# Hybrid NSA and gated DeltaNet block on one core: the padding tile in front of the activations grows from 224 to 288 bytes

## The chip, the cores and the metric

The kernel runs on one core of one Trainium2 chip. The metric is the device time in microseconds (us) of one execution. The engines are called by their short names: PE (TensorE, the products), PEld (its loading of weights), DVE (VectorE), ACT (ScalarE), POOL (GpSimd) and SP (SyncE, which issues most transfers).

## The reference

One layer of a decoder block over 256 tokens of 2,048 features, in float32. Cut to what matters here, it is a chain of large products with small mixers between them:

```python
proj = rms_norm(x, norm1_w) @ w_in
o_nsa = nsa_mixer(...)        # attention: compressed, selected and window branch, 8 heads
o_dn = gated_deltanet(...)    # linear attention, 8 heads, chunks of 64
mixed = g_nsa * (o_nsa @ w_up_nsa) + g_dn * (o_dn @ w_up_dn)
x = x + mixed @ w_o
h2 = rms_norm(x, norm2_w)
x = x + (silu(h2 @ w_ffn_gate) * (h2 @ w_ffn_up)) @ w_ffn_down
return rms_norm(x, norm_f_w)
```

All weights come from main memory, mostly 512 KB per transfer, and each is used for all 256 tokens at once. The hidden width of the FFN is 5,632.

## The kernel before

**How a product is made.** Every float32 operand is split into two parts, hi and lo, in the type that PE multiplies in one pass (float32r); a product of two operands is made of hi x hi, hi x lo and lo x hi. Weights arrive in six buffers called raw, ACT writes hi (L171), DVE writes lo = raw - hi (L172). There are three buffers hi of 4,096 bytes per partition and three buffers lo of 4,352. Activations are split once per stage and stay in memory for the whole of it.

**Two kinds of groups.** A product on PE has a stationary operand (128 columns, loaded as weights, PEld) and a moving operand that is streamed past it.
- `group_t` (transposed groups) holds hi or lo of the weights stationary and streams 256 tokens of activations. Its products are L248. Half a chunk is 24 of them: 16 with hi and 8 with lo. It makes most of the input projection (activations `hh`), the two up projections (`odn`, `onsa`) and the FFN's gate and up (`h2`, shown as `h` in the trace).
- Natural groups hold activations stationary and stream 512 columns of hi or lo: `products` (L1307, L1308, L1312) for `w_o` (activations `xa`, `leftw`) and for the FFN's down projection (`fa`, `fx`, `comb`, `leftsy`, `left1`, and the tiles `dd`), and `nat_mm` (L276, L277, L278) for the first groups (`zab`, 354 and 356 columns wide) and for `nsav`, with `hh` stationary. In some units seven products of blocks stand in place of eight; their combined weights are staged through main memory by the generator `staged`, in the tiles `stagew` and `stage`.
- The last products of all (`last_half`, L1663 to L1665) stream 256 columns of a tile `dd` past `fx`.

**The nudge.** After some transposes and other plain products the flag `nudge` is set. The next half chunk of `group_t` then writes its lo 16 elements (64 bytes) further into the buffer (the third argument of `split`, L242); the buffer has the room for it.

**The order of work.** PE's order is the order of the program. Small work (mixers, staging) stands in generators that `pump` advances by one step after each half chunk; `staged` lets six pumps pass between asking for a load and using it.

**Where the tiles lie.** Tiles are placed one behind the other along each partition, pool by pool, in the order of the pools: `wp` (raw, hi, lo), `cp` (constants, then the pad, then two tiles R), `sp` (small values), `hp` (`hh`, later `xa`, later `fa`: one piece of memory), `xy` (four tiles x, y, z, w that change their use), then `arena` (the mixers' memory) and in its place `pb` (`h2`, later `comb`; `dd`; temporaries). The pad is a tile that nothing reads or writes. By the sizes, with the pad at 56 floats, the addresses modulo 256 bytes are:

| behind the pad? | tiles | address modulo 256 |
|---|---|---|
| no | hi, lo | 128 |
| no | lo, nudged | 192 |
| yes | hh, h2, odn, onsa | 0 |
| yes | xa, fa, fx, comb | 64 |
| yes | leftw (two of three), leftsy, left1, dd, stage | 0 |
| yes | arena's main, stagew, x1t | 64 |

`hh` and `fa` share one piece of memory, but `four` starts `hh` at its beginning and `xa` and `fa` 16 elements further; `h2` and `onsa` are moved by 48 elements within their tiles, which start at 64.

Of the kernel before, what the change touches and what calls it, by code (L numbers as in the profile page):

```python
# [7 lines left out]
F32 = mybir.dt.float32  # L8
# [6 lines left out]
P = 128  # L15
# [84 lines left out]
class Kern:  # L100
# [885 lines left out]
    def build(self):  # L986
# [54 lines left out]

        xT = self.ar.alloc([16, 256], "x")
        sq = self.ar.alloc([4, 4, 256], "y")
        self.cp.tile([P, 56], F32, name="pad")
        hh = self.four(self.hp, "a", "hh", 16, 0)

        class First:
# [881 lines left out]
```

## Time and profile before

| what | value |
|---|---|
| median of 3 executions | 1484.56 us (1484.2 to 1484.64) |
| the profiled execution's own time | 1485.05 us |
| its span | 1483.3 us |
| PE busy | 1472.5 us, 99% |
| DVE, ACT, POOL busy | 1076.6, 749.2, 69.5 us |
| moved by DMA | 363.70 MB, 245 GB/s in the mean |

The span goes from the first instruction of the program to the last; the time of an execution has a little around it. Busy times count an engine's instructions where they overlap only once. The chain of work that ended last is followed back from the last instruction, at each step to what released it; its shares say which engine and line set the end. In the groups of instructions the mean length of a product is that of one in a pipeline, from its start to its modelled end; several are under way at a time, so the distance between two starts is shorter. In the list in order of time, each row has the start, the length, and how many instructions in succession were merged.

### The profile page before, as it was taken

The numbers are of one execution on the slowest core, as the hardware profiler recorded it, in microseconds if no ns is written. First come the engines' busy times: TensorE is split into PE (matmuls) and PEld (weight loads), VectorE is DVE, ScalarE is ACT, GpSimd is POOL, SyncE is SP. The second block draws the span as 40 slices with busy tenths as digits, with TensorE's granted clock in tenths as the row PEclk, the third lists the DMA queues.
The fourth block names the chain that finished last, engine by engine and source line by source line (L and its number), as shares of the span: only waits on it lengthen the run. The fifth ranks groups of instructions, "written<-read, shape, count | busy, mean of one in ns | idle before, by whom it ended". The sixth has DMA issues, their size and how long they took to land.

```text
span 1483.3 us, 27316 instructions
## 1 busy us (share of the span) xinstructions
PE 1472.5 (99%) x10937; PEld 1408.1 (95%) x10937; DVE 1076.6 (73%) x1645; ACT 749.2 (51%) x945; POOL 69.5 (5%) x62
## 2 busy tenths in 40 slices
PE   9999999999999999999999999999999999999997
PEld 9999999999999999998899999999999999888886
DVE  7668997767797755677876766666666556968777
ACT  6655444344445445445654444444344445766666
POOL 1000101000000000120000000000000000000000
PEclk9999999999999999999999999999999999999999
DMA  8765556357766457658778888888888655898895
GB/s 292 229 202 172 176 169 199 130 169 238 262 226 213 142 188 251 216 180 274 261 271 297 318 310 306 303 300 313 307 315 304 228 184 184 272 325 279 273 319 207
DMA packets 108462, 363.70 MB, mean 245 GB/s; under 512 B 12192, under 2 KB 12848, under 8 KB 104240
## 3 DMA queue, kind: packets, MB, share of 16 engines
q1 hardware_dynamic: 93264, 293.17, 58.7%
q10 hardware_dynamic: 13968, 66.17, 12.2%
q0 software_dynamic: 1104, 2.64, 0.7%
q8 instruction: 85, 1.39, 0.4%
q14 instruction: 41, 0.34, 0.1%
HBM read 327.57 MB, written 34.35 MB: 244 GB/s over the span
## 4 chain that ended last, share of the span: by engine, by line
PE 99%; DMA 0%; DVE 0%; SPq 0%; ACT 0%; issue 0%; DVEq 0%
PE mm L248 68%; PE mm L1307 6%; PE mm L1308 6%; PE mm L1312 6%; PE mm L277 2%; PE mm L276 2%; PE mm L278 2%; PE oacc L943 1%; PE U L613 1%; PE mmx L1312 1%; PE mmx L1308 1%; PE mmx L1307 1%; DMA raw<-in_zab 0%; PE pt L929 0%; PE hid L796 0%; PE hid L797 0%
## 5 line engine op out<-in xcount | busy, mean ns | idle before, releaser
L171 ACT ACTIVATE hi<-raw 128x1024 fp32r<-128x1024 f32 (+2 forms) x390 | 407.2, 1045 | 520.3 <-PE mm L248 413.5
L172 DVE TENSOR_TENSOR lo<-raw,hi 128x1024 fp32r<-128x1024 f32 (+2 forms) x390 | 469.9, 1205 | 232.8 <-ACT hi L171 231.2
L248 PE MATMUL mm<-h,hi 128*128 128x256 f32 x2816 | 363.4, 281 | 0.0
L248 PEld LDWEIGHTS mm<-h,hi 128*128 128x128 f32 x2816 | 346.6, 188 | 0.1
L248 PE MATMUL mm<-hh,hi 128*128 128x256 f32 x2304 | 300.3, 283 | 0.0
L248 PEld LDWEIGHTS mm<-hh,hi 128*128 128x128 f32 x2304 | 283.7, 188 | 0.6 <-ACT hi L171 0.4
L1288 DVE TENSOR_TENSOR lo<-raw,hi 128x1024 fp32r<-128x1024 f32 (+1 forms) x177 | 196.9, 1131 | 60.8 <-ACT hi L1287 56.5
L1287 ACT ACTIVATE hi<-raw 128x1024 fp32r<-128x1024 f32 (+1 forms) x177 | 173.1, 986 | 99.6 <-PE mm L1308 60.8
L248 PE MATMUL mm<-h,lo 128*128 128x256 f32 x1408 | 195.7, 281 | 0.0
L248 PEld LDWEIGHTS mm<-h,lo 128*128 128x128 f32 x1408 | 179.3, 188 | 0.0
L248 PE MATMUL mm<-hh,lo 128*128 128x256 f32 x1152 | 160.3, 281 | 0.0
L248 PEld LDWEIGHTS mm<-hh,lo 128*128 128x128 f32 x1152 | 146.7, 188 | 0.0
L1550 POOL TENSOR_TENSOR sgt<-sgt,R 128x512 f32<-128x512 f32 x22 | 35.3, 1603 | 546.9 <-ACT sgt L1549 546.9
L276 PE MATMUL mm<-hi,hh 128*128 128x354 f32 (+2 forms) x128 | 44.0, 350 | 1.2 <-ACT hi L158 1.2
L277 PE MATMUL mm<-lo,hh 128*128 128x354 f32 (+2 forms) x128 | 44.4, 347 | 0.0
L278 PE MATMUL mm<-hi,hh 128*128 128x354 f32 (+2 forms) x128 | 44.0, 344 | 0.0
L1307 PE MATMUL mm<-hi,fa 128*128 128x512 f32 x112 | 44.0, 393 | 0.0
L1308 PE MATMUL mm<-hi,fa 128*128 128x512 f32 x112 | 44.0, 392 | 0.0
L1307 PE MATMUL mm<-hi,comb 128*128 128x512 f32 x91 | 35.9, 394 | 0.0
L1308 PE MATMUL mm<-hi,comb 128*128 128x512 f32 x88 | 34.5, 392 | 0.0
L1400 POOL TENSOR_TENSOR main<-main 128x512 f32<-128x512 f32 x7 | 15.1, 2158 | 394.0 <-DVE main L1399 394.0
L248 PE MATMUL mm<-onsa,hi 128*128 128x256 f32 x256 | 33.0, 281 | 0.0
(550 smaller groups left out, 1745.7 us busy)
## 6 DMA issues: line engine op xcount, KB each, us to landing
raw<-in_wfg SPq DMA_DIRECT2D x176, 512.0 KB, 5.3
raw<-in_wmg SPq DMA_DIRECT2D x64, 512.0 KB, 3.7
raw<-in_wd SPq DMA_DIRECT2D x64, 512.0 KB, 5.2
raw<-in_wdn SPq DMA_DIRECT2D x48, 512.0 KB, 4.2
stage<-in_wd ACTq DMA_DIRECT2D x48, 512.0 KB, 6.8
scrD<-stage ACTq DMA_DIRECT2D x24, 1024.0 KB, 6.5
raw<-in_nsa SPq DMA_DIRECT2D x32, 512.0 KB, 3.5
raw<-in_wo SPq DMA_DIRECT2D x26, 512.0 KB, 4.9
```

The lines of the kernel that those rows point to most:

```text
L171: nc.scalar.activation(hv, v, AF.Copy)
L172: nc.vector.tensor_tensor(lv, v, hv.bitcast(F32), op=OP.subtract)
L248: nc.tensor.matmul(ps[:, f], (hv, hv, lv)[p][:, k, f * P:f * P + P], a[:, p % 2, :], start=c + h + p + k == 0, stop=c == n - 1 and h + p + ...
L276: nc.tensor.matmul(o, a[:, 0, sl], hv[:, k, :], start=begin, stop=False)
L277: nc.tensor.matmul(o, a[:, 0, sl], lv[:, k, :], start=False, stop=False)
L278: nc.tensor.matmul(o, a[:, 1, sl], hv[:, k, :], start=False, stop=last)
L1287: keep(nc.scalar.activation(hv, v, AF.Copy))
L1288: keep(V.tensor_tensor(lv, v, hv.bitcast(F32), op=OP.subtract))
L1307: nc.tensor.matmul(bank, ahi, hv[:, k, :], start=id(bank) not in begun, stop=False)
L1308: nc.tensor.matmul(bank, alo, hv[:, k, :], start=False, stop=False)
L1312: nc.tensor.matmul(bank, ahi, lv[:, k, :], start=False, stop=end)
L1550: nc.gpsimd.tensor_tensor(sgt[:], sgt[:], self.R2b, op=OP.mult)
```

## The change

The pad gets 16 floats more, 64 bytes per partition. Everything allocated behind it, that is R, the small values, the activations, the mixers' memory and the tiles that later take its place, moves by 64 bytes. raw, hi and lo and the first constants (`ident`, `n2t`, `ones`, `warm`, `n1t`) stay. `hh`, `h2`, `odn` and `onsa` then lie at 64 modulo 256 and `xa`, `fa`, `fx` and `comb` at 128. No instruction is added or removed.

```diff
         xT = self.ar.alloc([16, 256], "x")
         sq = self.ar.alloc([4, 4, 256], "y")
-        self.cp.tile([P, 56], F32, name="pad")
+        self.cp.tile([P, 72], F32, name="pad")
         hh = self.four(self.hp, "a", "hh", 16, 0)
```

## Prediction

> **What bounds the kernel now.** I read the first part of the page, then the chain of work that ended last, then single products on TensorE.
>
> ```profile
> PE 1472.5 (99%) x10937; PEld 1408.1 (95%) x10937; DVE 1076.6 (73%) x1645; ACT 749.2 (51%) x945; POOL 69.5 (5%) x62
> ...
> PEclk9999999999999999999999999999999999999999
> ...
> PE 99%; DMA 0%; DVE 0%; SPq 0%; ACT 0%; issue 0%; DVEq 0%
> PE mm L248 68%; PE mm L1307 6%; PE mm L1308 6%; PE mm L1312 6%; PE mm L277 2%; PE mm L276 2%; PE mm L278 2%; PE oacc L943 1%; PE U L613 1%; PE mmx L1312 1%; PE mmx L1308 1%; PE mmx L1307 1%; DMA raw<-in_zab 0%; PE pt L929 0%; PE hid L796 0%
> ```
>
> TensorE is never idle and its clock is granted in full. The span is therefore the number of products times the distance between the starts of two of them, which I call the pace. No engine or transfer beside TensorE sets the end, and the change removes no product. It can only change the pace. The time by line says where: L248, the transposed groups, has 68%; lines 1307, 1308 and 1312, the natural groups, some 20%.
>
> The pace of L248 comes from the chain of waits, which gives a long unbroken stretch as one piece, and the number of products from the busy time of that line over the whole span:
>
> ```profile
> 758.07 489.86 PE mm L248 x4128
> ```
> ```profile
> 0.00:1483.30 1483.30, 1014.97 (x8448) 1.00 0.72 245
> ```
>
> 489.86 us over 4,128 products is 118.67 ns each. 256 columns at this pace, and 8,448 such products in all, make 1,002 us. The length that the groups show for one product (281 ns) is a pipelined length and not the pace.
>
> **Which addresses meet.** A product streams its moving operand while the weights (the stationary operand) of the next one are loaded. I write "distance" for the address of the moving operand minus that of the stationary one, modulo 256 bytes. By the sizes of the tiles, laid end to end, hi and lo (all in front of the pad) start at 128; behind the pad hh, h2, odn and onsa start at 0, xa, fa, comb and fx at 64, leftw, leftsy, left1 and the dd tiles at 0. Everything behind the pad moves by 64, hi and lo stay.
>
> - L248 streams activations (0) past hi or lo (128): distance 128, which becomes 192.
> - Lines 1307 to 1312 stream hi or lo (128) past fa, xa, comb or fx (64): 64 becomes 0. Past leftw, leftsy, left1 and dd: 128 becomes 64.
> - A nudged lo starts at 192, so its distance 64 becomes 128.
>
> The trace of before has products at the new distances, since a few pair two tiles behind the pad. They keep their own distance and serve as samples.
>
> **Distance 192 at 256 columns** is what L248 will have. The last twelve products (dd streamed at 0 past fx at 64) run at it. First and last in order of time:
>
> ```profile
> 1473.02 0.28 PE L1663 MATMUL mmx<-dd,fx 128*128 128x256 f32 x1
> ...
> 1474.31 0.28 PE L1665 MATMUL mm<-dd,fx 128*128 128x256 f32 x1
> ```
>
> Eleven steps in 1.29 us are 117.3 ns; two digits behind the point leave 116.4 to 118.2. The nearest other row is a nudged group (distance 64), eight steps from 227.79 to 228.73, 117.5 ns:
>
> ```profile
> 227.79 1.10 PE L248 MATMUL mm<-hh,lo 128*128 128x256 f32 x8
> 228.73 0.52 PE L248 MATMUL mm<-hh,hi 128*128 128x256 f32 x3
> ```
>
> I take 117.7, in the upper half of the rows' interval since twelve products are few. That is 0.97 ns less for each of 8,448: **-8.2 us**. The lower bound is 116.4, or -19.2 us. The upper bound is the slowest pace that 256 columns show anywhere over eight steps or more, here at distance 128:
>
> ```profile
> 540.13 1.12 PE L248 MATMUL mm<-hh,hi 128*128 128x256 f32 x8
> 541.09 1.12 PE L248 MATMUL mm<-hh,lo 128*128 128x256 f32 x8
> 542.05 0.64 PE L248 MATMUL mm<-hh,hi 128*128 128x256 f32 x4
> ```
>
> Twice 0.96 us over eight are 120.0 ns, 1.33 more than now: +11.2 us for all.
>
> **512 columns.** Two stretches of 132 products each, both over comb and fa, so at the same addresses (distance 64); then 27 steps of distance 128, eight of distance 0 (comb streamed at 64 past fx at 64) and six of distance 192:
>
> ```profile
> 1289.24 0.40 PE L1307 MATMUL mm<-hi,comb 128*128 128x512 f32 x1
> ...
> 1320.04 0.39 PE L1307 MATMUL mm<-hi,dd 128*128 128x512 f32 x1
> ...
> 1402.88 0.39 PE L1307 MATMUL mm<-hi,comb 128*128 128x512 f32 x1
> ...
> 1433.10 0.39 PE L1307 MATMUL mm<-hi,dd 128*128 128x512 f32 x1
> ```
> ```profile
> 1272.56 0.39 PE L1307 MATMUL mm<-hi,left 128*128 128x512 f32 x1
> ...
> 1278.86 0.39 PE L1307 MATMUL mm<-hi,fa 128*128 128x512 f32 x1
> ...
> 1464.32 0.62 PE L1312 MATMUL mm<-comb,fx 128*128 128x512 f32 x2
> ...
> 1466.13 0.39 PE L1307 MATMUL mm<-dd,fx 128*128 128x512 f32 x1
> ...
> 1467.53 0.39 PE L1307 MATMUL mmx<-hi,fa 128*128 128x512 f32 x1
> ```
>
> 30.80 us over 132 are 233.3 ns, 30.22 us are 228.9: one distance holds either of two paces for a whole stretch, whichever it fell into. Distance 128: 6.30 us over 27, 233.3. Distance 0: 1.81 us over eight, 226.3 (225.0 to 227.5 by its digits). Distance 192: 1.40 us over six, 233.3. So the distance matters, and 0 has the shortest pace seen. How many of the products these are is read from the groups of L1307, which 1308 and 1312 repeat:
>
> ```profile
> L1307 PE MATMUL mm<-hi,fa 128*128 128x512 f32 x112 | 44.0, 393 | 0.0
> L1307 PE MATMUL mm<-hi,comb 128*128 128x512 f32 x91 | 35.9, 394 | 0.0
> L1307 PE MATMUL mm<-hi,xa 128*128 128x512 f32 x83 | 32.7, 394 | 0.0
> L1307 PE MATMUL mm<-hi,fx 128*128 128x512 f32 x33 | 12.9, 391 | 0.0
> L1307 PE MATMUL mm<-hi,leftsy 128*128 128x512 f32 x26 | 10.2, 394 | 0.0
> L1307 PE MATMUL mm<-hi,leftw 128*128 128x512 f32 x26 | 10.3, 396 | 0.0
> ```
>
> The first four are 319, three lines 957, and some 10% more write the bank that the trace calls mmx: about 1,050 go from 64 to 0. I take 229.6 for now (between 228.9 and 233.3, nearer the first) and 226.9 for then, in the upper half again: -2.7 x 1,050 = **-2.8 us**. If they lock at 233.3 instead: +3.9 us. The others, with left1 and dd about 250, and 96 of nsav, go from 128 to 64: 233.3 to 229.6, **-1.3 us**, with +0 as the bound where they stay at 233.3.
>
> **The rest.** The 288 products of 354 and 356 columns in zab alternate between two distances, 128 and 8 or 16:
>
> ```profile
> 43.04 0.33 PE L276 MATMUL mm<-hi,hh 128*128 128x356 f32 x1
> ...
> 44.02 0.32 PE L276 MATMUL mm<-hi,hh 128*128 128x356 f32 x1
> ...
> 44.98 0.60 PE L1084 MATMUL R<-ident,rstd 128*128 128x128 f32 x4
> ```
>
> Six steps take 0.98 us (163 ns), the next six 0.96 (160). Their new distances are 64 and about 200; I take nothing, with 3 ns either way as bounds, +-0.9 us. Plain fp32 products between two tiles behind the pad keep their distance. ACT and DVE have the same instructions, and TensorE covers them. DMA destinations behind the pad move too: stage from 0 to 64. stagew lies at 64 already:
>
> ```profile
> stage<-in_wd ACTq DMA_DIRECT2D x48, 512.0 KB, 6.8
> stagew<-in_wo ACTq DMA_DIRECT2D x4, 512.0 KB, 7.2
> ```
>
> 0.4 us more for a load is hidden by the six pumps that the generator waits, each 24 products of 118.67 ns, 17 us together. If that cover went, 48 loads would cost 19 us at most. The Trainium skill ("DMA: Bandwidth & Descriptors", section "How a descriptor splits into AXI transactions") says that a descriptor which doesn't start on a 256-byte boundary takes an additional transaction; the 0.4 us agrees in sign, and it leaves the sum as it is.
>
> **The sum.** -8.2 - 2.8 - 1.3 = -12.3 us. The profiled execution took 1485.05 us (span 1483.3 and 1.75 around it), 0.5 above the median of 1484.56. From its time 1472.8, from the median 1472.3. First products after every restart don't hold the pace yet; I write 1473.
>
> **Rivals.**
> *A worse lock (slower).* L248 falls, at a restart after transposes, into the 120.0 pace or its like and stays for the stretch, as the 132 products at 233.3 did. For it: 512 columns at distance 192 show the slowest pace, 233.3; one stretch of L248 has 4,128 products, so one bad start decides half; and the nudge, which ahead of some stretches now changes the distance to 64 for eight products, will change it to 128, where the 120.0 was seen. Against it: at 256 columns of L248's rows only this one stretch of some 20 products is quoted with it, against 4,128 without, and the twelve at distance 192 did not have it. Price: +11.2 - 4.1 = 1491.6 us; with 233.3 in the 512 columns too, 1499.6. It decides once more than 0.6 of L248's products run so (12.3 of 8.2 + 11.2).
>
> *No change.* The paces belong to the stages and their history, not to addresses, or the pad is swallowed by rounding. For it: hh, h2, odn and onsa, four tiles, have one pace, but they also have one address modulo 256. Against it: comb past fx takes 226.3 where dd past fx, the same shapes a moment later, takes 233.3. Rounding can't swallow it, since the tiles behind the pad stand at odd multiples of 64 too. Time: 1484.6. The Trainium skill ("SBUF — State Buffer", section "Who interferes with whom") gives TensorE two independent read ports, one for the moving operand and one for weights, and says it never waits on anyone. By that rule the addresses could not matter and the change would do nothing; the pair of rows just named disagrees.
>
> *Half of it.* L248 gains 8.2, the 512 columns lock at 233.3 (+3.9, +0): 1480.3 us.
>
> **Chances.** Forecast 0.50, half of it 0.10, no change 0.10, worse lock 0.27; 0.03 for a mixture of both signs, a third to each side. A measurement of this kernel tells 0.2% (3 us) from no change. Faster 0.61, same 0.11, slower 0.28. The forecast's own range is 1464 (116.4 for L248 would give 1461.3) to 1478. The range that leaves out no more than 2 in 10 goes up to the worse lock with its price: 1465 to 1493.
>
> **What would show it.** The stretch of L248 that now is x4128 with 489.86 us would be 486 at 117.7 and 495 at 120.0, and unchanged if addresses don't matter. The 132 products over comb and fa would take 29.95 us at 226.9. TensorE would stay at 99% in the chain; a share of DMA there above 0% would say that the faster stream uncovered the loads, and I would be wrong in calling them hidden. The forecast falls if the long stretch is longer than 489.9.

## The result and the profile after

The changed kernel takes 1441.75 us (median of 5 executions, 1441.32 to 1444.0). The kernel before, on the same chip and between them, takes 1484.2 us (1483.82 to 1484.64). The ratio is 0.9717, with a 95% interval of 0.9702 to 0.9731: 42 us or 2.8% faster. The forecast was 1473.0 with a range down to 1465, so the sign is right and the size is not: the gain is more than three times the 12 us that were worked out. The profiled execution took 1441.32 us, with a span of 1439.5.

The page of the changed kernel: busy times, and the chain that ended last by engine and line.

```profile
PE 1428.2 (99%) x10937; PEld 1366.6 (95%) x10937; DVE 1075.0 (75%) x1645; ACT 748.5 (52%) x945; POOL 69.7 (5%) x62
...
PE 97%; DVE 1%; DMA 1%; ACT 0%; issue 0%; SPq 0%; DVEq 0%; ACTq 0%
```

The same products, with TensorE as busy as before: what fell is the pace. The span by three stages (up to the long stretch of L248, that stretch, and the rest), first of the kernel before and then of the changed one. A row has the stretch, its length, then the busy time and number of instructions of PE, PEld, DVE, ACT and POOL, the granted clock, the DMA's share and GB/s:

```profile
0.00:758.07 758.07, 755.94 (x5821) 733.19 (x5822) 577.52 (x1073) 389.46 (x541) 34.23 (x40) 1.00 0.63 210
758.07:1247.93 489.86, 489.86 (x4129) 489.86 (x4129) 315.40 (x347) 206.45 (x214) 35.27 (x22) 1.00 0.82 285
1247.93:1483.30 235.37, 226.66 (x990) 185.10 (x989) 183.69 (x226) 153.27 (x191) 0.00 (x0) 0.99 0.81 276
```
```profile
0.00:739.11 739.11, 736.51 (x5821) 713.86 (x5822) 576.54 (x1073) 388.89 (x541) 34.27 (x40) 1.00 0.64 215
739.11:1207.09 467.98, 467.98 (x4129) 467.98 (x4129) 315.38 (x347) 206.62 (x214) 35.46 (x22) 1.00 0.85 299
1207.09:1439.50 232.41, 223.68 (x990) 184.73 (x989) 183.12 (x226) 153.01 (x191) 0.00 (x0) 0.99 0.83 279
```

The clock is granted in full in both. The saving is 18.96 us before the long stretch, 21.88 in it, and 2.96 in the natural groups behind it, 43.8 together. By line, over the whole span of the changed kernel, L248 (busy time of that line, products, clock, DMA):

```profile
0.00:1439.50 1439.50, 974.05 (x8448) 1.00 0.74 253
```

That is 40.9 us less than the 1014.97 of before. So L248 alone has 93% of the saving of the profiled executions. Its pace is read from the chain, for the kernel before and for the changed one (start, length, number):

```profile
61.40 60.00 PE mm L248 x504
566.86 91.12 PE mm L248 x768
```
```profile
61.07 57.40 PE mm L248 x504
413.82 5.66 PE mm L248 x48
...
425.91 5.46 PE mm L248 x48
...
551.98 87.33 PE mm L248 x768
739.11 467.98 PE mm L248 x4128
```

The long stretch now has 467.98 / 4,128 = 113.37 ns per product, where 117.7 was forecast. The stretches of 48 show two paces side by side: 5.66 / 48 = 117.9 and 5.46 / 48 = 113.8. The forecast's sample, the twelve products dd past fx, still has the slower one in this very execution, first and last in order of time:

```profile
1429.19 0.28 PE L1663 MATMUL mmx<-dd,fx 128*128 128x256 f32 x1
...
1430.49 0.28 PE L1665 MATMUL mm<-dd,fx 128*128 128x256 f32 x1
```

Eleven steps take 1.30 us, 118 ns. Distance 192 thus has at least two paces at 256 columns, and the sample showed the one that most of L248 did not take.

The switch can be seen. Around the start of the long stretch (after), four plain products for R are followed by 16 products with hi, the eight with the nudged lo, and the rest:

```profile
738.86 2.13 PE L248 MATMUL mm<-h,hi 128*128 128x256 f32 x16
740.83 1.11 PE L248 MATMUL mm<-h,lo 128*128 128x256 f32 x8
741.78 1.88 PE L248 MATMUL mm<-h,hi 128*128 128x256 f32 x15
```

Eight nudged products take 0.95 us (118.8 ns). By the starts in the trace, the first step of the stretch takes 200 ns and the next 14, ahead of the nudge, 117.9 each. From the fourth product behind the nudged ones to the end, 4,100 steps, each takes 113.33.

The natural groups went as forecast. The 132 products over comb and fa, first product and the one behind the last:

```profile
1247.88 0.39 PE L1307 MATMUL mm<-hi,comb 128*128 128x512 f32 x1
...
1277.79 0.39 PE L1307 MATMUL mm<-hi,dd 128*128 128x512 f32 x1
```

29.91 us over 132 are 226.6 ns; the forecast had 29.95. In the list of what TensorE waited for, the changed kernel has one row that the kernel before has not (us in total, times, longest):

```profile
...
PE x1T L1435 <- DVE x1t L1427: 0.8, 1, 0.8
```

The transposes of x1T now come 0.8 us before DVE has finished x1t. No wait on a transfer is in the list, though loads land later than before (stage 7.1 us in place of 6.8). The chain passes through one more load, near the end. The row of the issues, and that of the chain:

```profile
stage<-in_wd ACTq DMA_DIRECT2D x48, 512.0 KB, 7.1
```
```profile
1407.25 6.86 DMA raw<-in_wd
```

### The profile page after: what moved, and what is told of

Same layout as the page of the kernel before. It is cut to its first block, busy times and chain, and to the rows that moved or that the text cites. A ratio compares the mean times of both kernels' runs of the same rounds, so it can differ in the third digit from the quotient of the medians.

```text
span 1439.5 us, 27316 instructions
## 1 busy us (share of the span) xinstructions
PE 1428.2 (99%) x10937; PEld 1366.6 (95%) x10937; DVE 1075.0 (75%) x1645; ACT 748.5 (52%) x945; POOL 69.7 (5%) x62
## 4 chain that ended last, share of the span: by engine, by line
PE 97%; DVE 1%; DMA 1%; ACT 0%; issue 0%; SPq 0%; DVEq 0%; ACTq 0%
PE mm L248 67%; PE mm L1307 6%; PE mm L1308 6%; PE mm L1312 6%; PE mm L277 2%; PE mm L276 2%; PE mm L278 2%; PE oacc L943 1%; PE U L613 1%; PE mmx L1312 1%; PE mmx L1308 1%; PE mmx L1307 1%; DMA raw<-in_wd 0%; DMA raw<-in_zab 0%; PE pt L929 0%; PE hid L796 0%
## 5 line engine op out<-in xcount | busy, mean ns | idle before, releaser
L248 PE MATMUL mm<-h,hi 128*128 128x256 f32 x2816 | 348.5, 276 | 0.0
L248 PEld LDWEIGHTS mm<-h,hi 128*128 128x128 f32 x2816 | 332.6, 188 | 0.1
L248 PE MATMUL mm<-hh,hi 128*128 128x256 f32 x2304 | 290.4, 279 | 0.0
L248 PEld LDWEIGHTS mm<-hh,hi 128*128 128x128 f32 x2304 | 274.6, 188 | 0.6 <-ACT hi L171 0.4
L248 PE MATMUL mm<-h,lo 128*128 128x256 f32 x1408 | 188.3, 276 | 0.0
L248 PEld LDWEIGHTS mm<-h,lo 128*128 128x128 f32 x1408 | 172.7, 188 | 0.0
L248 PE MATMUL mm<-hh,lo 128*128 128x256 f32 x1152 | 155.3, 277 | 0.0
L248 PEld LDWEIGHTS mm<-hh,lo 128*128 128x128 f32 x1152 | 142.3, 188 | 0.0
L1307 PE MATMUL mm<-hi,xa 128*128 128x512 f32 x83 | 32.6, 393 | 0.0
```

Source lines behind the costliest of these rows:

```text
L248: nc.tensor.matmul(ps[:, f], (hv, hv, lv)[p][:, k, f * P:f * P + P], a[:, p % 2, :], start=c + h + p + k == 0, stop=c == n - 1 and h + p + ...
L1307: nc.tensor.matmul(bank, ahi, hv[:, k, :], start=id(bank) not in begun, stop=False)
```

## The experiments

The open question was why L248 gained five times its term. Theory: the distance decides among a few paces, and distance 192 has a faster one, 113.3, beside the 117.7 of the sample. Rivals: the faster pace belongs to the place of the activations or to engines and transfers beside TensorE, not to the distance; or L248's pace settles with time and has nothing to do with how a stretch starts.

**Products alone.** The block is left out: the program only streams products, and its output is a copy of half of x. Stretches of 96 products at eight distances, then stretches behind one to eight transposes at four distances.

```python
for d in range(0, 256, 32):
    cols256(d, 96, ...)        # 96 products of 256 columns, moving operand at distance d
    plain(4)                   # four transposes
...
for d in range(0, 256, 64):
    for e in range(1, 9):
        plain(e)
        cols256(d, 48, ...)
```

> This kernel leaves the whole block out: it copies half of x to both halves of the output and beside that only streams products on TensorE, with no other engine at work meanwhile. The stationary tile starts at 128 modulo 256; eight moving tiles start 0, 32, ... 224 bytes further, and each is streamed for 96 products of 256 columns, then 96 of 512. After that distances 0, 64, 128 and 192 again, with 1 to 8 plain transposes ahead of every stretch, so that stretches begin at different moments. Theory (the distance between moving and stationary address sets which paces exist, the moment of the start chooses among them): 256 columns at distance 192 show both 113.3 and 117.8 ns, depending on the number of transposes; at 128 they show 118.7 or 120.0 and never 113.3; 512 columns at 0 show 226.7, at 192 233.3, at 64 228.9 or 233.3. Rival (the paces come from other engines and transfers that touch the memory at the same time): all distances have one pace here, near 109 ns, which 256 columns at full clock would need with no loss (106.7 and little more).

The chain of this run, in order of time: distances 64, 128 and 192 at 256 columns; three of 512 columns (distances 0, 64, 192); then distance 192 behind one, four and eight transposes.

```profile
35.37 11.31 PE n256d L62 x96
...
59.06 11.52 PE n256d L62 x96
...
82.72 10.90 PE n256d L62 x96
...
105.86 21.81 PE n512d L69 x96
...
150.94 21.99 PE n512d L69 x96
...
241.88 22.40 PE n512d L69 x96
...
436.37 5.66 PE e1n256d L62 x48
...
454.32 5.46 PE e4n256d L62 x48
...
479.00 5.46 PE e8n256d L62 x48
```

Distance 192 has the shortest stretch of all, 10.90 / 96 = 113.5 ns with its entry, against 117.8 at distance 64 and 120.0 at 128. Behind one to three transposes (5.66 us each) it runs at 117.9, behind four to eight (5.46 each) at 113.8, entry included. No other engine works during these stretches and transfers move 1 GB/s, and both paces are there all the same: the rival that blames the neighbours falls. In this run the pace goes with the number of transposes just ahead; the finer scan further down does not repeat that. At 512 columns the order is that of the forecast: 0, then 64, then 192.

**The weights moved instead.** The activations stay where they were; raw, hi and lo move by 192 bytes, which gives L248 the same distance. The edits of this kernel and of the next two are shown against the kernel before, those further down against the changed kernel.

```diff
+        self.wp.tile([P, 48], F32, tag="front", bufs=1, name="front")
-        self.cp.tile([P, 56], F32, name="pad")
+        self.cp.tile([P, 8], F32, name="pad")
```

> The pad goes back to 8 floats and 48 floats are put in front of raw, hi and lo instead: everything behind the pad stands where it stood before (hh at 0, fa at 64), and raw, hi and lo start at 64 instead of 128. The distances are those of the changed kernel (192 for L248, 0 for lines 1307 to 1312 past fa, xa, comb, fx). Theory (distance alone): 1441 to 1444 us, and L248 at 113.3 ns in its long stretch. Rival (the place of the activations, or of the mixers' memory and staging tiles behind the pad, does it): 1484 us, as nothing behind the pad has moved.

```profile
740.04 467.98 PE mm L248 x4128
```

1442.24 us, ratio to the kernel before 0.9714 (0.9698 to 0.9731): the same gain and the same length of the long stretch, to the hundredth. So for this move the difference of the two addresses decides; where the activations lie by themselves makes no difference that can be measured.

**Two other distances.** The pad at 88 floats gives L248 distance 0 and the 512 columns over xa, fa and comb 192; at 40 floats it is 64 and 128.

```diff
-        self.cp.tile([P, 56], F32, name="pad")
+        self.cp.tile([P, 88], F32, name="pad")     # the other kernel: 40
```

> Another 64 bytes of pad (88 floats): distance 0 for L248, 192 for the 512 columns past fa, xa, comb and fx, 0 past leftw, leftsy, left1 and dd. Theory: 512 columns at 233.3 (6 us more than in the changed kernel); for L248 only four products of before ran at distance 0, around 116 to 120 ns, so 1440 to 1500 us. Rival (what counts is that the activations left 0 modulo 256): about 1442 us.

> 64 bytes of pad less than before (40 floats): distance 64 for L248, 128 for the 512 columns past fa, xa, comb and fx, 192 past leftw, leftsy, left1 and dd. Theory: 512 columns at 232 to 233.3; L248 in the 117.5 that the nudged groups of before showed, or in a quicker pace that eight products were too few to reach: 1440 to 1478 us. Rival (what counts is that the activations left 0 modulo 256): about 1442 us.

The chains, of 88 and of 40:

```profile
762.18 495.33 PE mm L248 x4128
```
```profile
60.83 57.44 PE mm L248 x504
558.16 87.41 PE mm L248 x768
746.25 486.21 PE mm L248 x4128
```

With 88 the kernel is 0.8% slower than before, 1496.99 us, 1.0084 (1.0064 to 1.0104): the pace is 120.0, the prediction's "worse lock", at another distance. With 40 it takes 1471.57 us in the profiled execution and 1453.39 in the other, 0.9851 (0.9781 to 0.9922). The rows say why the two can lie 18 us apart: within one execution the stretches of 504 and 768 run at 113.8 to 114.0 with their entries, the long one at 117.8, and 4,128 products at 113.4 in its place would be 18 us less. So distance 64 also holds two paces. That the long stretch had the faster one in the shorter execution fits these numbers, but no trace of that execution shows it.

**Without the nudge ahead of the long stretch.** If a stretch keeps the pace that it starts with, the nudge is what moves the long one from 117.8 to 113.33.

```diff
             R2 = row_bcast(r2, "R2")
-            self.nudge = True
```

> The changed kernel without one thing: the nudge in bcast2, ahead of the long stretch of the FFN, so that no eight products past a lo at another address stand in it. In the changed kernel the 15 products ahead of that nudge start 117.8 ns apart and the 4,105 behind it 113.33. Theory (distance 192 holds two paces at 256 columns, a stretch takes one at its restart and holds it, and only a break such as the nudge moves it): all 4,128 stay at 117.8, x4128 with 486 us in the chain, and the kernel takes 1441.8 + 4,113 x 4.45 ns = 1460. Rival (the slower pace is a start-up state that dies out by itself, and the nudge has nothing to do with it): 1441.8, x4128 with 468.

Chain and order of time of this run:

```profile
740.15 486.19 PE mm L248 x4128
```
```profile
739.91 2.13 PE L248 MATMUL mm<-h,hi 128*128 128x256 f32 x16
741.87 1.11 PE L248 MATMUL mm<-h,lo 128*128 128x256 f32 x8
```

1460.4 us (1458.48 to 1460.63), ratio 0.9835 (0.982 to 0.9849); 1460 was expected. The rows up to the lo are those of the changed kernel, an equal 2.13 us for the first sixteen; the long stretch then stays at 486.19 / 4,128 = 117.8 to its end. Here the slower pace is taken at the start, holds for half a millisecond, and does not settle by itself. That rival falls.

**Without any nudge.**

```diff
-                hv, lv = self.split(rv[h], 256, 16 * self.nudge)
+                hv, lv = self.split(rv[h], 256, 0)
```

> The changed kernel without any nudge: no lo is ever moved 64 bytes on. In the changed kernel eight stretches (96, 49, 145, 145, 96, 745 and 4,105 products among them) run at 113.33 behind a nudge although the 15 products ahead of it ran at 117.8; together some 5,400 products. Theory (as for the run without the FFN's nudge): they stay at 117.8, +24 us, 1465.8, and x768 takes 90.4 us in place of 87.3. Rival (the pace settles by itself): 1441.8.

```profile
61.17 57.34 PE mm L248 x504
553.32 90.46 PE mm L248 x768
742.90 486.19 PE mm L248 x4128
```

1463.75 us (1463.6 to 1463.95), 0.986 (0.9844 to 0.9876), 2 us less than expected. x768 falls to the slower pace too (90.46; expected 90.4), x504 keeps the faster without its nudge, and so does one stretch of 168 that was counted on to slow down. Of the 42 us that the change brought, some 22 (1463.75 - 1441.75) need the nudges that were already there beside the new distance; with the distance alone the kernel takes 1463.75.

**Finer distances.** Products alone again, the block left out: 256 columns at 32 distances in steps of 8 bytes, behind four and behind two transposes, and 512 columns in steps of 16.

```python
w = sb.tile([P, 2112], F32R, name="mov")
dist = {d: w[:, d // 4:d // 4 + 2048] for d in range(0, 256, 8)}
for e in 4, 2:
    for d in dist:
        plain(e)
        cols256(d, 64, ...)
```

> Only products, with the block left out: the output is a copy of half of x. Stretches of 64 products of 256 columns at 32 distances, in steps of 8 bytes from 0 to 248, once behind four transposes and once behind two; then 48 products of 512 columns at 16 distances in steps of 16. Theory (the distance modulo 256 sets the pace on a grid of 6.67 ns, and 113.33 is its lowest step seen): 192 gives 113.3 behind four and 117.8 behind two transposes, as in the first stretches of products alone; no distance gives less than 113.3 at 256 columns or less than 226.7 at 512. Rival (the steps of 32 bytes missed the best place, and 256 columns can go at 106.7 to 110 with a finer one): some distance between 160 and 224 gives under 112 ns; then the kernel's pad is to be moved there. Second rival (only the 64-byte line counts): eight neighbours within 64 bytes have one pace.

The chain: behind four transposes the distances 112, 120 and 192, then behind two the distance 112.

```profile
125.10 7.32 PE e4n256d L61 x64
132.86 7.79 PE e4n256d L61 x64
...
205.81 7.54 PE e4n256d L61 x64
...
380.27 7.32 PE e2n256d L61 x64
```

7.32 us is the shortest of the 64 rows, and both are distance 112: 113.33 ns after the entry, behind four and behind two. Its neighbour eight bytes on, 120, takes 7.79, so it is not the 64-byte line that counts. Nothing at 256 columns goes below 113.3, nothing at 512 below the 226.7 of distance 0. Distance 192 had 117.8 behind four transposes here, where 113.3 was expected and the first run of products alone had 113.4: the number of transposes alone doesn't select the pace. The two programs also differ in where the moving tile lies and in what ran before.

**Distance 112 in the kernel.** A version meant to beat the changed kernel: L248 at 112, xa, fa, comb, fx, leftw, leftsy and the second dd at 0, no nudge.

```diff
-        self.cp.tile([P, 72], F32, name="pad")
-        hh = self.four(self.hp, "a", "hh", 16, 0)
+        self.cp.tile([P, 48], F32, name="pad")
+        hh = self.four(self.hp, "a", "hh", 80, 4)
...
-        xa = self.quarters(xat, 16)
+        xa = self.quarters(xat, 40)
```

> All products are kept. The activations that the transposed groups stream are put at distance 112 (pad 48 floats, and offsets of 4 or 52 in their tiles), xa, fa, comb, fx, leftw, leftsy and the second dd at distance 0 by larger offsets, and no lo is nudged. In the finer scan 112 gave 113.3 ns at 256 columns behind four and behind two transposes, where 192 gave 117.8 behind both. Theory (112 has the one pace 113.3, whatever the restart): every stretch of L248 at 113.3 without nudges. Against the changed kernel that is some 620 products behind restarts and 104 nudged ones at 4.4 to 5.6 ns less each, -3.3 us; some 170 products past leftw, leftsy and dd at 2.2 ns less, -0.4; nsav at 144 in place of 64, +0.4; left1 +0.2; zab unknown, -1 to +1. In all 1438.5, x4128 with 468 us, x768 with 87.1. Rival (112 has two paces as 64 and 192 have): without nudges the long stretch may fall into 117.8, 1457 and more.

> The changed kernel as it is, on the same chip and beside the same runs as the kernel with distance 112, so that a difference of a few us between the two can be read. Theory (the nudge brings the long stretch into 113.33 each time): 1441.8 in every execution, x4128 with 468 us. Rival (it is chance from execution to execution, as at distance 64): some executions near 1460.

Distance 112, the chain, and the busy time of L248 over the span; then the changed kernel beside it, both views:

```profile
427.21 5.50 PE mm L248 x48
...
739.69 467.90 PE mm L248 x4128
```
```profile
0.00:1441.00 1441.00, 972.81 (x8448) 1.00 0.74 252
```
```profile
740.78 467.98 PE mm L248 x4128
```
```profile
0.00:1441.00 1441.00, 974.85 (x8448) 1.00 0.74 252
```

The theory holds: without a nudge the long stretch runs at 467.90 / 4,128 = 113.35, and the starts in the trace show every shorter one reaching 113.3. But the time is the same, 1441.65 us against 1441.92; their ratios to the kernel before are 0.9711 (0.9698 to 0.9724) and 0.971 (0.9697 to 0.9724). L248 gave 2.0 of the 3.3 us expected, since behind a restart up to 14 products, mostly 115 to 122 ns apart, go by before the pace is reached, and the natural stage at the end lost 1.2 (233.41 us in place of 232.24). The changed kernel took 1440.29 to 1442.85 in five executions, none near 1460: the times leave no room for a long stretch in the slower pace, which would cost 18 us. This version does not beat it by a measurable amount.

Shorter stretches do change. One stretch of 96 products without a nudge, in the first profiled execution of the changed kernel and in this one:

```profile
368.71 10.89 PE mm L248 x96
```
```profile
369.49 11.30 PE mm L248 x96
```

That is 113.4 and 117.7 ns each, at distance 192, behind the same instructions of the same program. So the pace at a restart is not fixed by the program alone. Behind the nudge, the long stretch had the faster one in both executions.

## Why the prediction was right or wrong

*That the pace sets the time, and that the distance bears on the pace: right, though one distance does not fix one pace.* The weights moved in place of the activations gave the same time, and the paces stand in a program that does nothing but products. "No change" falls with it. The Trainium skill ("SBUF — State Buffer", section "Who interferes with whom") says that TensorE's two read ports are independent and that it never waits on anyone. The section does not speak of addresses. Taken as the prediction takes it, as a rule by which they could not matter, the rows disagree: with all other engines idle the same product took 113.5 to 120.0 ns by the difference of its two addresses.

*Distance 192 at 256 columns, -8.2 us: the step that failed.* It measured -40.9. The sample was read correctly, and it still runs at 118 ns in the changed kernel; but one sample of twelve products was taken for the pace of the distance, and "the lower bound is 116.4" was only that sample's rounding. The prediction had seen, in the 512 columns, that "one distance holds either of two paces for a whole stretch", and it used this only toward the slow side, as the worse lock. Applied to both sides it would have made the lower bound open, since no row of the profile before shows the faster pace for this distance. Even the 1461.3 us that the prediction works out from its lower bound is 20 us above the measured time. A bound drawn from one short stretch is no bound for 4,128 products that start elsewhere.

*The natural groups, -2.8 and -1.3: right.* The 132 products took 29.91 us (29.95 forecast). A run of 21 products over leftsy, whose distance went from 128 to 64, took 4.90 us before and 4.81 after, 233 and 229 ns each, as forecast. All that isn't L248 gained 43.8 - 40.9 = 2.9 us against 4.1, and the new wait of 0.8 us on x1t is in it.

*The worse lock (0.27): the mechanism exists, the place was wrong.* L248 does hold a pace for a whole stretch, and the nudge does decide it for the long one, as the prediction feared; but here it moved the long stretch to the faster one. The 120.0 pace came at distance 0, with 1496.99 us.

*Loads stay covered: right.* No transfer stands among TensorE's waits, with 299 GB/s in the long stretch in place of 285 and somewhat later landings. DMA rose to 1% of the chain, which the prediction had named as the sign of uncovered loads. It isn't one here: the load that joined the chain (6.86 us at 1407) lies in the last stage, where TensorE's idle time is 8.7 us before and after (235.37 - 226.66 and 232.41 - 223.68). That loads into the tile stage land 0.3 us later need not be the price of its new boundary, to which the prediction's comparison of 6.8 and 7.2 us points. With the weights moved, stage lies at 0 modulo 256 as before and its loads took longer; with the pad at 88 it lies at 128 and they took less. The rows of these two:

```profile
stage<-in_wd ACTq DMA_DIRECT2D x48, 512.0 KB, 7.3
```
```profile
stage<-in_wd ACTq DMA_DIRECT2D x48, 512.0 KB, 6.6
```

*Where the gain came from, in one line:* 21.9 us from the 4,128 products, 19.0 ahead of them, 3.0 behind, of which some 22 us only because the nudges that were already there bring these stretches into the faster pace.

## What to carry to other kernels

Where TensorE is never idle, compare the starts of its products stretch by stretch: several paces for one shape mean that the addresses of the moving and the stationary operand, modulo 256 bytes, are worth a scan with a program of products alone, which costs one run. Measure a distance from several restarts and over long stretches before a price is put on it, because one distance can hold two paces, and here a long stretch kept the one that it had taken. A few products at another distance, as the nudge makes them, can move a stretch from the slower to the faster.

## What had not been expected of the hardware

- At 256 columns distances 64 and 192 hold 113.3 or 117.8 ns, distance 112 held only 113.3, and distance 0 held 120.0; at 512 columns distance 0 has 226.7, 64 has 228.9 (and 233.3 in one stretch of the kernel before) and 192 has 233.3. 113.33, 120.0, 226.67 and 233.33 are 17, 18, 34 and 35 times 6.667 ns; 117.8 is 17 2/3 of it, as a repeating pattern of three steps in the trace's starts. What lies behind this step isn't shown by these runs.
- The pace of a stretch held for 4,100 steps without a slip, beside ACT, DVE and transfers of 299 GB/s.
- What selects the pace at a restart stays open. It isn't the number of transposes ahead (four gave 113.4 in one run of products alone and 117.8 in the other), and a stretch of 96 in the kernel had 113.4 in one execution and 117.7 in another.
- The Trainium skill ("TensorE: Matmul & The Clock Gate", section "Back-to-back issue gap") gives N / 2.4 + 2.5 ns as the gap of an isolated product of N columns on a full clock, which makes an estimate of 109.2 ns at 256 columns and 215.8 at 512; for a stream of products it gives less than that at 512. No stretch here reached either figure of the formula: the shortest were 113.3 and 226.7.
